# MLP up projections of a two-layer encoder: tokens on partitions in sets of 512 columns, turned by VectorE blocks and SP moves

## The chip, the cores and the metric

The kernel runs on one core of one Trainium2 chip. The metric is the device time in microseconds (us) of one execution, as the median of several runs. The core has TensorE (PE: matrix products into PSUM), VectorE (DVE), ScalarE (ACT), GpSimd (POOL) and SyncE (SP), whose queue issues the DMA transfers here.

## The reference

Two layers on 256 tokens of 1024 channels. Each layer has a token mixer (pooling, attention, gates; not touched here) and then this MLP, with a depthwise convolution of width 3 over the tokens on the branch `a`:

```python
D_MODEL, SEQ, DEPTH, D_FF, CONV_WIDTH, EPS = 1024, 256, 2, 2816, 3, 1e-6

def _conv_ffn(xn, w_up, conv_w, conv_b, w_down):
    a, gval = jnp.split(xn @ w_up, 2, axis=-1)
    a = lax.conv_general_dilated(a, conv_w[:, None, :], window_strides=(1,),
                                 padding=((CONV_WIDTH // 2, CONV_WIDTH // 2),),
                                 dimension_numbers=('NWC', 'WIO', 'NWC'),
                                 feature_group_count=D_FF) + conv_b
    return (jax.nn.gelu(a) * gval) @ w_down

for layer in range(DEPTH):
    h = h + _token_mixer(_rmsnorm(h, norm1[layer]), ...)
    h = h + _conv_ffn(_rmsnorm(h, norm2[layer]), w_up[layer], conv_w[layer], conv_b[layer], w_down[layer])
return _rmsnorm(h, norm_f)
```

All is float32. The kernel computes GELU in its tanh form.

## The kernel before

**Numbers and weights.** Each float32 operand is split into a high and a low part of type fp32r (`wh`, `wl` for weights; two parts of the activations), and a product is three matmuls: high by high, high by low, low by high. Class `Weights` streams the weights in the order in which `use` names the pieces: a load of 1 MB on SP's queue (line 119) fills a tile `raw`, of which three exist; each load is cut in two pieces; ScalarE copies a piece to `wh` (line 179), VectorE subtracts to get `wl` (line 180). Five pairs of `wh` and `wl` exist. `get` hands the next piece to TensorE and has the pieces up to three further ahead split; `_split` issues the loads that fit. A piece counts 128 x 1024 values, whatever its shape: 1024 rows by 128 columns for a column projection, 512 by 256 for rows, and so on. The program issues its instructions in the order of its text; each engine runs its own list in order, and a scheduler between the text and these lists may shift an instruction within its engine's list.

**Two ways to multiply by the up weights.** DFF is 22 chunks of 128 columns; each chunk has an `a` and a `g` half. A *column projection* (`proj`, `two_sums`, lines 485 and 487) holds a 1024 x 128 piece as the fixed operand and streams the 256 tokens: 8 matmuls of 512 columns (both parts of the tokens behind one another), then 8 of 256. Its result has channels on partitions and tokens along the row, as the convolution wants it. *By rows* (`v_sum`, line 582) the tokens are the fixed operand and 512 columns of weights stream; the result has tokens on partitions. One quarter of such a group (one piece, 256 of the 1024 input channels, six matmuls for each of two halves of the tokens, 12 in all) is called a unit below. The tokens stand in two halves, even and odd, `t` = 0 and 1.

**The MLP before.** The `a` of the last four chunks (18 to 21) is computed by rows; its first half is started by `begin_values` at the end of the phase before, to bridge the last norm there. ScalarE copies it out, and VectorE turns it by 32 x 32 blocks that it writes straight to other partitions (`blocks`, line 612). Everything else is a column projection: for each chunk `up(f)` takes `a` (18 times) and `g` (22 times), 40 projections in each layer. `add_up` (lines 507 and 508) lets ScalarE copy one of the two sums out of PSUM and VectorE add the other. Convolution, GELU and the product with `g` follow on ScalarE and VectorE, and the result is split in two parts for the down product.

**Down product and end.** `residual_mm` is a generator with one step per chunk: each of the first 18 steps runs 12 matmuls of 512 columns (lines 512 to 514) into four PSUM tiles; the last four pieces are only held. After them each segment of the result (two of 512 columns for half 0; 512, 256 and 256 for half 1) gets its 12 held matmuls and goes to `Norm.add` (line 417: the sum into `h`; line 419: squares), and in the first layer `fin` of `to_channels` normalises (line 444) and TensorE transposes (line 453); in the last layer `store` scales and writes out. Two chunks of `up` alternate with two steps of `down`, which stay `LAG` = 6 chunks behind.

**Moves.** `cross` (line 604) issues 16 DMAs on SP that carry 32-partition blocks to other partitions, four per step. Attention uses it already (tiles `pt`, 64 KB each, and `way`).

Of the kernel before, what the change touches and what calls it, by code (L numbers as in the profile page):

```python
# [10 lines left out]
F32 = mybir.dt.float32  # L11
F32R = mybir.dt.float32r
AF = mybir.ActivationFunctionType
ALU = mybir.AluOpType
AX = mybir.AxisListType

P = 128
D = 1024
S = 256
# [7 lines left out]
DFF = 2816  # L27
NF = DFF // P
# [7 lines left out]

WARM = (5, 1, 2, 1)
PAIRS = (2, 4, 0, 1, 3, 5)
LAG = 6
VISITS = ((0, 1, 12, 14), (2, 3, 15, 16), (9, 10, 22, 23), (10, 11, 23, 24))  # L40
ENTRY = 4
FIRST = NF - ENTRY
HALVES = (slice(0, 512), slice(512, D))
SEGMENTS = (HALVES, (slice(0, 512), slice(512, 768), slice(768, D)))

# [37 lines left out]
class Weights:  # L83
# [27 lines left out]
    def load(self, upto):  # L111
        while self.n_loaded < min(upto, len(self.loads)):
            src, shape, tag = self.loads[self.n_loaded]
            name = f"raw{self.n_loaded}"
            if tag is None:
                t = self.pool.tile([P, *shape], F32, tag="raw", bufs=self.RAW, name=name)
            else:
                t = self.idle.tile([P, *shape], F32, tag=tag, name=name)
            self.nc.sync.dma_start(out=t, in_=src)
            self.raw[self.n_loaded] = t  # L120
            self.n_loaded += 1

# [84 lines left out]
def encoder(ctx, tc, x, w_in, w_pool, pool_scale, w_a, w_b, w_o, norm1, norm2, w_up, conv_w,  # L207
            conv_b, w_down, rel_bias, norm_f, onehot, edges, out):
    nc = tc.nc
    const = ctx.enter_context(tc.tile_pool(name="const", bufs=1))  # L210
    wpool = ctx.enter_context(tc.tile_pool(name="weights", bufs=1))
    big = ctx.enter_context(tc.tile_pool(name="big", bufs=1))
# [6 lines left out]
    W = Weights(tc, wpool, big)  # L219

    def cols(w, c0):

        src = w[:, c0 : c0 + 256].rearrange("(k p) c -> p k c", p=P)
        return W.add(
            src, (8, 256), [((lambda t, j=j: t[:, :, j * P : (j + 1) * P]), (8, P)) for j in (0, 1)]
        )

    def rows(w, r0, n=2, c0=0, width=1024, tag=None, pieces=2):

        src = w[r0 : r0 + n * P, c0 : c0 + width].rearrange("(k p) c -> p k c", p=P)  # L230
        h = n // pieces
        return W.add(
            src, (n, width), [((lambda t, j=j: t[:, j * h : (j + 1) * h, :]), (h, width)) for j in range(pieces)],
            tag,
        )

    for l in range(DEPTH):
        for g in range(NG):
            c0 = C_V + g * 512
            slots = (("m2", 0, 2), ("m2", 1, 2), ("ybig",), ("at2",)) if g == 0 else ()  # L240
            for j in range(2):
                tag = "k1" if l == 0 and g == 1 and j == 0 else None
                W.use(rows(w_in[l], j * 512, 4, c0, 512, tag), slots[2 * j : 2 * j + 2])
        if l == 0:
            W.n_scaled = len(W.pieces)
        for c in range(3, -1, -1):
            W.use(cols(w_in[l], c * 256))
        for n, c in enumerate(PAIRS):
            q = cols(w_in[l], C_Q + c * 256)
            if n == 1:  # L250
                pool = W.add(
                    w_pool[l].rearrange("g (k p) c -> p (g k) c", p=P), (8, 256),
                    [((lambda t, j=j: t[:, 4 * j : 4 * j + 4, :]), (4, 256)) for j in range(2)],
                )
            k = cols(w_in[l], C_K + c * 256)
            if n == 1:
                k.insert(1, pool[0])
            if n == 2:
                q.insert(1, pool[1])
            W.use(q + k)  # L260
        def half_of(w, c0, half, n):
            for j in range(n):
                W.use(rows(w, j * 512, 4, c0 + half.start, 512))

        for half in HALVES:
            half_of(w_in[l], C_GP, half, 2)
        for half in HALVES:
            half_of(w_a[l], 0, half, 2)
            half_of(w_in[l], C_GA, half, 2)
            half_of(w_b[l], 0, half, 1)  # L270
        for c in range(4):
            W.use(rows(w_o[l], c * 256))
        slots = (("v1",), ("ybig",), ("at2",))
        for j in range(2):
            W.use(rows(w_up[l], j * 512, 4, FIRST * P, 512), slots[2 * j : 2 * j + 2])
        for f in range(0, NF, 2):
            a = cols(w_up[l], f * P) if f < FIRST else []
            g = cols(w_up[l], DFF + f * P)
            W.use([a[0], g[0], a[1], g[1]] if a else g)
            if f >= LAG:  # L280
                W.use(rows(w_down[l], (f - LAG) * P))
        for f in range(NF - LAG, NF, 2):
            W.use(rows(w_down[l], f * P))


    h = const.tile([P, 2, D], F32, name="h")
# [210 lines left out]
    def halves(a):  # L497

        return a.rearrange("p (t m) -> p t m", t=2)

    def in_order(a):

        return a.rearrange("p (m t) -> p t m", t=2)

    def add_up(out, sums):

        nc.scalar.copy(out=out, in_=sums[1])
        nc.vector.tensor_add(out=out, in0=sums[0], in1=out)  # L508
# [65 lines left out]
    def v_tile():  # L574
        return acc.tile([P, 512], F32, tag="acc", name="v_ps")

    def v_sum(ps, x2, t, n, piece, of=4):

        _, (wh, wl) = piece
        passes = [(0, wh, 0), (0, wl, 0), (1, wh, 0), (0, wh, 1), (0, wl, 1), (1, wh, 1)]  # L580
        for m, (part, w, j) in enumerate(passes):
            nc.tensor.matmul(  # L582
                ps, x2[:, 2 * n + j, part, t, :], w[:, j, :], start=(n + m == 0),
                stop=(n == of - 1 and m == 5),
            )
# [21 lines left out]
    def blocks(out, in_):  # L607

        for i in range(4):
            for j in range(4):  # L610
                a, b = slice(32 * i, 32 * i + 32), slice(32 * j, 32 * j + 32)
                nc.vector.transpose(out=out[b, :, :, a], in_=in_[a, :, :, b])
                yield
# [166 lines left out]
    for l in range(DEPTH):  # L780
# [326 lines left out]
        acts = {}  # L1107


        a_last = big.tile([P, ENTRY, S], F32, tag="gates", name="a_last")  # L1110
        a_rows = big.tile([P, 2, ENTRY, P], F32, tag="m2", name="a_rows")

        held, ps = entry
        for t in range(2):
            if t:
                ps = v_tile()
                for n in range(4):
                    v_sum(ps, x2, t, n, held[n])
            nc.scalar.copy(out=a_rows[:, t], in_=ps)
        for i, _ in held:  # L1120
            W.free(i)
        turning = blocks(a_last.rearrange("p f (m t) -> p t f m", t=2), a_rows)

        def up(f):
            w0, w1, w2, b = (prm[:, l, j * NF + f : j * NF + f + 1] for j in range(4))
            if f >= FIRST:
                a = a_last[:, f - FIRST, :]
            else:
                a = sm.tile([P, S], F32, tag="u", name="a")
                add_up(in_order(a), [halves(b) for b in proj(x2)])  # L1130
                next(turning, None)
            sums = proj(x2)
            y = sm.tile([P, S], F32, tag="s", name="y")
            nc.scalar.activation(y, a, AF.Identity, bias=b, scale=w1)  # L1134
            nc.vector.scalar_tensor_tensor(
                out=y[:, 1:], in0=a[:, : S - 1], scalar=w0, in1=y[:, 1:], op0=ALU.mult, op1=ALU.add
            )
            nc.vector.scalar_tensor_tensor(
                out=y[:, : S - 1], in0=a[:, 1:], scalar=w2, in1=y[:, : S - 1],
                op0=ALU.mult, op1=ALU.add,  # L1140
            )
            g = sm.tile([P, 2, P], F32, tag="p", bufs=3, name="g")
            add_up(g, [halves(a) for a in sums])

            c = float(np.sqrt(2.0 / np.pi))
            y2 = sm.tile([P, S], F32, tag="us", name="y2")
            nc.scalar.activation(y2, y, AF.Square, scale=float(np.sqrt(0.044715)))
            nc.vector.scalar_tensor_tensor(  # L1148
                out=y2, in0=y2, scalar=1.0, in1=y, op0=ALU.add, op1=ALU.mult
            )  # L1150
            nc.scalar.activation(y2, y2, AF.Tanh, scale=c)  # L1151
            nc.vector.scalar_tensor_tensor(
                out=y2, in0=y2, scalar=1.0, in1=y, op0=ALU.add, op1=ALU.mult
            )
            nc.vector.scalar_tensor_tensor(
                out=g, in0=in_order(y2), scalar=0.5, in1=g, op0=ALU.mult, op1=ALU.mult
            )
            n = f % NH
            ah, al = (x[n >= HPG][:, n - HPG * (n >= HPG)] for x in (acth, actl))
            nc.scalar.copy(out=ah, in_=g)  # L1160
            nc.vector.tensor_sub(out=al, in0=g, in1=ah.bitcast(F32))
            acts[f] = (ah, al)

        late = {}
# [11 lines left out]
            lambda k: acts[k], NF, lambda *a: late["norm"].add(*a),  # L1176
            fill=begin_values if l + 1 < DEPTH else None,
        )
        for f in range(0, NF, 2):
            up(f)  # L1180
            up(f + 1)
            if f >= LAG:
                next(down)
                next(down)
        if l + 1 < DEPTH:
            x2 = two_parts("x", "x2")
            late["norm"] = Norm(to_channels(x2, mmp, g1))
# [33 lines left out]
```

## Time and profile before

| | |
|---|---|
| median of 3 runs | 870.25 us (870.25 to 870.68) |
| profiled execution, its own time | 870.25 us |
| its span in the trace | 868.5 us |
| mean granted clock of TensorE | 0.998 |
| DMA: mean rate over the span | 193 GB/s |

PE is TensorE's matmuls, PEld its loads of the fixed operand, which overlap them. SPq rows are instructions on SP's queue; a row with x8 stands for eight in succession. In rows of the timeline the first two numbers are the start and the length, both in us. In the list of groups the columns are busy time, mean ns of one, then idle time of the engine just before them and what ended most of it. In the view by tile a row gives the shortest, median and longest duration in ns and the time of the first and last start.

### The profile page before, as it was taken

How to read it: one execution, taken by the hardware profiler on the slowest of the kernel's cores; microseconds unless marked ns; L12 is line 12 of the kernel's file. 1: busy time of each engine (PE TensorE's matmuls, PEld its weight loads, DVE VectorE, ACT ScalarE, POOL GpSimd, SP SyncE). 2: the span in 40 equal slices, each digit the busy share in tenths (PEclk: the TensorE clock that was granted, in tenths of full speed). 3: DMA queues.
4: the chain of work that ended last, by engine and by line, in shares of the span. 5: the costliest groups of instructions: out<-in, count | busy, mean ns of one | idle time of the engine just before them, and what ended most of it. 6: DMA issues, size and time to landing. Idle time of an engine off the chain costs nothing.

```text
span 868.5 us, 12204 instructions
## 1 busy us (share of the span) xinstructions
PE 860.7 (99%) x4554; PEld 740.9 (85%) x4554; DVE 670.5 (77%) x1084; ACT 496.8 (57%) x817; POOL 21.1 (2%) x53
## 2 busy tenths in 40 slices
PE   9999999999999999999999999999999999999997
PEld 7888988888888888888888899888888888888885
DVE  6998795756759997789756968775557799887884
ACT  6755644544646775667545555454445467666662
POOL 2020000000010000000000000000000000000000
PEclk9999999999999999999999999999999999999999
DMA  9676636664745565555626455547558255664631
GB/s 326 210 210 229 223 118 223 189 222 158 270 155 194 185 203 193 197 193 194 242 98 225 163 195 194 173 167 241 186 203 274 96 183 200 223 205 155 198 141 49
DMA packets 116095, 167.23 MB, mean 193 GB/s; under 512 B 4846, under 2 KB 81854, under 8 KB 116036
## 3 DMA queue, kind: packets, MB, share of 16 engines
q1 hardware_dynamic: 115524, 165.12, 56.6%
q0 software_dynamic: 496, 1.33, 0.6%
q8 instruction: 36, 0.59, 0.3%
q14 instruction: 23, 0.19, 0.1%
q10 hardware_dynamic: 16, 0.00, 0.0%
HBM read 160.12 MB, written 1.07 MB: 186 GB/s over the span
## 4 chain that ended last, share of the span: by engine, by line
PE 99%; ACT 0%; POOLq 0%; DVE 0%; issue 0%; POOL 0%; ACTq 0%
PE proj_ps L485 30%; PE rows_ps L582 18%; PE proj_ps L487 16%; PE res_ps L512 6%; PE res_ps L513 6%; PE v_ps L582 6%; PE res_ps L514 6%; PE v_ps L772 3%; PE v_ps L685 1%; PE o_ps L963 1%; PE s_ps L906 1%; PE o_ps L959 1%; PE s_ps L901 1%; PE xt_ps L453 1%; PE pool_ps L479 0%; PE pool_ps L478 0%
## 5 line engine op out<-in xcount | busy, mean ns | idle before, releaser
L180 DVE TENSOR_TENSOR wl<-raw,wh 128x1024 fp32r<-128x1024 f32 x274 | 333.1, 1222 | 121.0 <-ACT wh L179 118.4
L179 ACT CAST wh<-raw 128x1024 fp32r<-128x1024 f32 x274 | 285.6, 1049 | 173.0 <-PE proj_ps L485 64.7
L485 PE MATMUL proj_ps<-x,wh 128*128 128x512 f32 x1152 | 288.4, 392 | 0.0
L485 PEld LDWEIGHTS proj_ps<-x,wh 128*128 128x128 f32 x1152 | 208.2, 189 | 38.0
L487 PEld LDWEIGHTS proj_ps<-x,wl 128*128 128x128 f32 x1152 | 157.2, 190 | 11.3
L487 PE MATMUL proj_ps<-x,wl 128*128 128x256 f32 x1152 | 160.8, 282 | 0.0
L582 PE MATMUL rows_ps<-wh,x 128*128 128x512 f32 x256 | 82.1, 393 | 0.0
L512 PE MATMUL res_ps<-wh,actq 128*128 128x512 f32 (+1 forms) x184 | 70.2, 381 | 0.0
L513 PE MATMUL res_ps<-wl,actq 128*128 128x512 f32 (+1 forms) x184 | 70.1, 381 | 0.0
L514 PE MATMUL res_ps<-wh,actk 128*128 128x512 f32 (+1 forms) x184 | 69.9, 380 | 0.0
L582 PEld LDWEIGHTS rows_ps<-wh,x 128*128 128x128 f32 x256 | 47.9, 188 | 9.7
L582 PE MATMUL rows_ps<-wl,x 128*128 128x512 f32 x128 | 49.9, 389 | 0.0
L514 PEld LDWEIGHTS res_ps<-wh,actk 128*128 128x128 f32 x184 | 34.6, 188 | 6.7
L582 PE MATMUL rows_ps<-wh,po 128*128 128x512 f32 x128 | 40.1, 389 | 0.0
L512 PEld LDWEIGHTS res_ps<-wh,actq 128*128 128x128 f32 x184 | 34.7, 188 | 6.2
L513 PEld LDWEIGHTS res_ps<-wl,actq 128*128 128x128 f32 x184 | 34.7, 188 | 6.0
L1134 ACT ACTIVATE y<-a,prm 128x256 f32<-128x256 f32 x36 | 21.6, 600 | 21.9 <-DVE a L508 21.9
L1151 ACT ACTIVATE y<-y 128x256 f32<-128x256 f32 x44 | 18.3, 416 | 21.4 <-DVE y L1148 21.2
L582 PEld LDWEIGHTS rows_ps<-wh,po 128*128 128x128 f32 x128 | 24.0, 188 | 5.0
L582 PEld LDWEIGHTS rows_ps<-wl,x 128*128 128x128 f32 x128 | 24.1, 188 | 4.8
L512 PE MATMUL res_ps<-wh,m 128*128 128x512 f32 (+1 forms) x72 | 26.9, 374 | 0.0
L419 ACT ACTIVATE junk<-h 128x512 f32<-128x512 f32 (+1 forms) x20 | 10.9, 547 | 27.1 <-DVE h L417 27.1
(209 smaller groups left out, 1155.0 us busy)
## 6 DMA issues: line engine op xcount, KB each, us to landing
raw<-in_w_in_dram SPq DMA_DIRECT2D x58, 1024.0 KB, 5.2
raw<-in_w_up_dram SPq DMA_DIRECT2D x44, 1024.0 KB, 4.9
raw<-in_w_down_dram SPq DMA_DIRECT2D x22, 1024.0 KB, 4.9
raw<-in_w_a_dram SPq DMA_DIRECT2D x8, 1024.0 KB, 5.8
raw<-in_w_o_dram SPq DMA_DIRECT2D x8, 1024.0 KB, 7.1
pt<-rows SPq DMA_DIRECT2D x64, 64.0 KB, 3.7
raw<-in_w_b_dram SPq DMA_DIRECT2D x4, 1024.0 KB
raw<-in_w_pool_dram SPq DMA_DIRECT2D x2, 1024.0 KB
```

The source lines that it names most:

```text
L179: lambda: nc.scalar.copy(out=h, in_=src),
L180: lambda: nc.vector.tensor_sub(out=l, in0=src, in1=h.bitcast(F32)),
L419: nc.scalar.activation(junk[:, 0 : cc.stop - cc.start], h[:, t, cc], AF.Square, scale=D**-0.5, accum_out=ss[:, n : n + 1],)
L485: nc.tensor.matmul(ps, wh(k), x2[:, k], start=(k == 0), stop=False)
L487: nc.tensor.matmul(ps[:, 1], wl(k), x2[:, k, 0], start=False, stop=(k == nk - 1))
L512: nc.tensor.matmul(ps, ah, wh, start=first, stop=False)
L513: nc.tensor.matmul(ps, ah, wl, start=False, stop=False)
L514: nc.tensor.matmul(ps, al, wh, start=False, stop=last)
L582: nc.tensor.matmul(ps, x2[:, 2 * n + j, part, t, :], w[:, j, :], start=(n + m == 0), stop=(n == of - 1 and m == 5),)
L772: nc.tensor.matmul(ps[t], a[:, k, t, :], w[:, j, :], start=(k + m == 0), stop=(k == KD - 1 and m == 2),)
L1134: nc.scalar.activation(y, a, AF.Identity, bias=b, scale=w1)
L1151: nc.scalar.activation(y2, y2, AF.Tanh, scale=c)
```

## The change

All up projections are now by rows. A group is 512 columns: a0 to a4 and g0 to g4 are four chunks of `a` or `g` each, r5 holds the last two chunks of both (two column ranges of 256, loaded by two DMAs from one entry, hence the tuple in `Weights.load`). `ORDER` lists the groups and the steps of the down product, d0 to d4, of four chunks each; chunks 20 and 21 are done in the end. a0 is the one that `begin_values` starts.

`turn_up` turns a finished group: VectorE transposes 32 x 32 blocks out of PSUM, one instruction for each half of the tokens (128 x 512), into `rows`, and `cross` carries the blocks with 16 DMAs of 32 KB on SP's queue to the tile `out`. The moves go out four per unit: `unit`, called after every unit and every down step, takes the next step of the oldest `cross`, and computes each chunk whose number in `CHUNKS` has been passed. `up` finds `a` and `g` turned in SBUF: ScalarE copies `a` into the order of tokens, and the product of GELU and `g` reads `g` where it is. The factor 0.5 moves from that product into the split that follows it, which becomes `scalar.mul` and one `scalar_tensor_tensor`. For each layer 40 column projections of 16 matmuls become 40 units of 12; the matmuls of the down product do not change.

```diff
--- before.py
+++ after.py
@@ -36,10 +36,9 @@
 
 WARM = (5, 1, 2, 1)
 PAIRS = (2, 4, 0, 1, 3, 5)
-LAG = 6
+ORDER = "a0 g0 a1 g1 a2 g2 d0 a3 g3 d1 a4 g4 r5 d2 d3 d4"
+CHUNKS = (13, 15, 17, 19, 21, 23, 25, 27, 29, 31, 33, 35, 41, 43, 45, 47, 53, 54, 56, 57, 58, 60)
 VISITS = ((0, 1, 12, 14), (2, 3, 15, 16), (9, 10, 22, 23), (10, 11, 23, 24))
-ENTRY = 4
-FIRST = NF - ENTRY
 HALVES = (slice(0, 512), slice(512, D))
 SEGMENTS = (HALVES, (slice(0, 512), slice(512, 768), slice(768, D)))
 
@@ -116,7 +115,9 @@
                 t = self.pool.tile([P, *shape], F32, tag="raw", bufs=self.RAW, name=name)
             else:
                 t = self.idle.tile([P, *shape], F32, tag=tag, name=name)
-            self.nc.sync.dma_start(out=t, in_=src)
+            parts = [(t[:, :, j], one) for j, one in enumerate(src)] if type(src) is tuple else [(t, src)]
+            for out, one in parts:
+                self.nc.sync.dma_start(out=out, in_=one)
             self.raw[self.n_loaded] = t
             self.n_loaded += 1
 
@@ -271,16 +272,27 @@
         for c in range(4):
             W.use(rows(w_o[l], c * 256))
         slots = (("v1",), ("ybig",), ("at2",))
-        for j in range(2):
-            W.use(rows(w_up[l], j * 512, 4, FIRST * P, 512), slots[2 * j : 2 * j + 2])
-        for f in range(0, NF, 2):
-            a = cols(w_up[l], f * P) if f < FIRST else []
-            g = cols(w_up[l], DFF + f * P)
-            W.use([a[0], g[0], a[1], g[1]] if a else g)
-            if f >= LAG:
-                W.use(rows(w_down[l], (f - LAG) * P))
-        for f in range(NF - LAG, NF, 2):
-            W.use(rows(w_down[l], f * P))
+        for kind, n in ORDER.split():
+            n = int(n)
+            for j in range(2):
+                if kind == "d":
+                    W.use(rows(w_down[l], (4 * n + 2 * j) * P))
+                elif kind == "r":
+                    src = w_up[l][j * 512 : (j + 1) * 512].rearrange("(k p) c -> p k c", p=P)
+                    c0 = (4 * n * P, 4 * n * P + DFF)
+                    W.use(
+                        W.add(
+                            tuple(src[:, :, c : c + 256] for c in c0), (4, 2, 256),
+                            [
+                                ((lambda t, j=j: t[:, 2 * j : 2 * j + 2].rearrange("p k h c -> p k (h c)")), (2, 512))
+                                for j in (0, 1)
+                            ],
+                        )
+                    )
+                else:
+                    p = rows(w_up[l], j * 512, 4, (kind == "g") * DFF + 4 * n * P, 512)
+                    W.use(p, slots[2 * j : 2 * j + 2] if (kind, n) == ("a", 0) else ())
+        W.use(rows(w_down[l], (NF - 2) * P))
 
 
     h = const.tile([P, 2, D], F32, name="h")
@@ -1107,29 +1119,40 @@
         acts = {}
 
 
-        a_last = big.tile([P, ENTRY, S], F32, tag="gates", name="a_last")
-        a_rows = big.tile([P, 2, ENTRY, P], F32, tag="m2", name="a_rows")
-
-        held, ps = entry
-        for t in range(2):
-            if t:
-                ps = v_tile()
-                for n in range(4):
-                    v_sum(ps, x2, t, n, held[n])
-            nc.scalar.copy(out=a_rows[:, t], in_=ps)
-        for i, _ in held:
-            W.free(i)
-        turning = blocks(a_last.rearrange("p f (m t) -> p t f m", t=2), a_rows)
+        turned, ways = {}, []
+
+        def turn_up(key, ps, tag):
+
+            if not ways:
+                for own in ("at2", "xn"):
+                    t = big.tile([P, 2, 4, 2, 4, 32], F32, tag=own, name="up_" + own)
+                    ways.append([t[:, 0], t[:, 1]])
+                ways.append([])
+            rows = ways[0].pop(0)
+            ways[0].append(rows)
+            if tag is None:
+                out = ways[1].pop(0)
+                ways[1].append(out)
+            else:
+                out = big.tile([P, 4, 2, 4, 32], F32, tag=tag, name="up_turned")
+            for t in range(2):
+                nc.vector.transpose(
+                    out=rows[:, :, t].rearrange("p j c r -> p c j r"),
+                    in_=ps[t].rearrange("p (c j r) -> p c j r", c=4, j=4),
+                )
+            ways[2].append(cross(out, rows))
+            turned[key] = out.rearrange("p i t c r -> p c t i r")
+
+        def blocks_in_order(a):
+
+            return a.rearrange("p (i r t) -> p t i r", i=4, t=2)
 
         def up(f):
             w0, w1, w2, b = (prm[:, l, j * NF + f : j * NF + f + 1] for j in range(4))
-            if f >= FIRST:
-                a = a_last[:, f - FIRST, :]
-            else:
-                a = sm.tile([P, S], F32, tag="u", name="a")
-                add_up(in_order(a), [halves(b) for b in proj(x2)])
-                next(turning, None)
-            sums = proj(x2)
+            n, c = divmod(f, 4)
+            av, gv = (turned["r", n][:, j + c] if n == 5 else turned[k, n][:, c] for k, j in (("a", 0), ("g", 2)))
+            a = sm.tile([P, S], F32, tag="u", name="a")
+            nc.scalar.copy(out=blocks_in_order(a), in_=av)
             y = sm.tile([P, S], F32, tag="s", name="y")
             nc.scalar.activation(y, a, AF.Identity, bias=b, scale=w1)
             nc.vector.scalar_tensor_tensor(
@@ -1139,8 +1162,6 @@
                 out=y[:, : S - 1], in0=a[:, 1:], scalar=w2, in1=y[:, : S - 1],
                 op0=ALU.mult, op1=ALU.add,
             )
-            g = sm.tile([P, 2, P], F32, tag="p", bufs=3, name="g")
-            add_up(g, [halves(a) for a in sums])
 
             c = float(np.sqrt(2.0 / np.pi))
             y2 = sm.tile([P, S], F32, tag="us", name="y2")
@@ -1152,13 +1173,14 @@
             nc.vector.scalar_tensor_tensor(
                 out=y2, in0=y2, scalar=1.0, in1=y, op0=ALU.add, op1=ALU.mult
             )
-            nc.vector.scalar_tensor_tensor(
-                out=g, in0=in_order(y2), scalar=0.5, in1=g, op0=ALU.mult, op1=ALU.mult
-            )
+            g = sm.tile([P, 2, P], F32, tag="p", bufs=3, name="g")
+            nc.vector.tensor_mul(out=g.rearrange("p t (i r) -> p t i r", i=4), in0=blocks_in_order(y2), in1=gv)
             n = f % NH
             ah, al = (x[n >= HPG][:, n - HPG * (n >= HPG)] for x in (acth, actl))
-            nc.scalar.copy(out=ah, in_=g)
-            nc.vector.tensor_sub(out=al, in0=g, in1=ah.bitcast(F32))
+            nc.scalar.mul(out=ah, in_=g, mul=0.5)
+            nc.vector.scalar_tensor_tensor(
+                out=al, in0=g, scalar=0.5, in1=ah.bitcast(F32), op0=ALU.mult, op1=ALU.subtract
+            )
             acts[f] = (ah, al)
 
         late = {}
@@ -1176,12 +1198,38 @@
             lambda k: acts[k], NF, lambda *a: late["norm"].add(*a),
             fill=begin_values if l + 1 < DEPTH else None,
         )
-        for f in range(0, NF, 2):
-            up(f)
-            up(f + 1)
-            if f >= LAG:
-                next(down)
-                next(down)
+        count, chunk = 0, 0
+
+        def unit():
+            nonlocal count, chunk
+            count += 1
+            if ways and ways[2] and next(ways[2][0], "end") == "end":
+                ways[2].pop(0)
+                if ways[2]:
+                    next(ways[2][0])
+            while chunk < NF and CHUNKS[chunk] < count:
+                up(chunk)
+                chunk += 1
+
+        for kind, n in ORDER.split():
+            if kind == "d":
+                for _ in range(4):
+                    next(down)
+                    unit()
+                continue
+            if (kind, n) == ("a", "0"):
+                held, ps = entry
+                ps = [ps, v_tile()]
+                for k in range(4):
+                    v_sum(ps[1], x2, 1, k, held[k])
+                    unit()
+                for i, _ in held:
+                    W.free(i)
+            else:
+                ps = by_rows(x2, 4, unit)
+            n = int(n)
+            turn_up((kind, n), ps, None if kind == "g" else ("gates", "v0")[n % 2])
+        assert chunk == NF
         if l + 1 < DEPTH:
             x2 = two_parts("x", "x2")
             late["norm"] = Norm(to_channels(x2, mmp, g1))
```

## The prediction

> **What bounds the kernel now.** First the page, for which engine sets the end.
>
> ```profile
> span 868.5 us, 12204 instructions
> PE 860.7 (99%) x4554; PEld 740.9 (85%) x4554; DVE 670.5 (77%) x1084; ACT 496.8 (57%) x817; POOL 21.1 (2%) x53
> PEclk9999999999999999999999999999999999999999
> PE 99%; ACT 0%; POOLq 0%; DVE 0%; issue 0%; POOL 0%; ACTq 0%
> ```
>
> The chain of waits is TensorE for 99% of the span, at an undisturbed clock. Busy matmuls overlap, so a gap could hide in that figure; the table by stretch, here for layer 0 from the first column projection of the MLP to the start of layer 1, and the timeline of TensorE in one round show that none does.
>
> ```profile
> core 0: us, PE busy (x) PEld busy (x) DVE busy (x) ACT busy (x) POOL busy (x), PEclk, DMA share, GB/s
> 263.66:436.18 172.52, 172.52 (x926) 149.29 (x924) 150.27 (x266) 112.76 (x201) 1.61 (x4) 1.00 0.59 201
> ...
> 347.02 1.98 PE L485 MATMUL proj_ps<-x,wh 128*128 128x512 f32 x8
> 348.83 1.12 PE L487 MATMUL proj_ps<-x,wl 128*128 128x256 f32 x8
> 349.79 2.00 PE L485 MATMUL proj_ps<-x,wh 128*128 128x512 f32 x8
> ...
> 358.17 0.40 PE L512 MATMUL res_ps<-wh,actq 128*128 128x512 f32 x1
> ...
> 363.41 0.39 PE L514 MATMUL res_ps<-wh,actk 128*128 128x512 f32 x1
> 363.63 0.39 PE L485 MATMUL proj_ps<-x,wh 128*128 128x512 f32 x1
> ```
>
> TensorE is busy in 172.52 of 172.52 us. Four column projections stand between 347.02 and 358.17: 11.15 us, 2.79 each. Then 24 matmuls of 512 columns take 358.17 to 363.63: 5.46 us, 0.2275 each. So the MLP costs what TensorE needs to stream it, and each idle moment that the change brings to TensorE is paid in full.
>
> **The stream: a gain.** A column projection streams 8 x 512 and 8 x 256 columns in 16 matmuls; a quarter of a group by rows (a "unit") streams the same columns in 12 matmuls of 512. At 0.2275 a unit is 2.73 us, a group of four 10.92 against 11.15. Ten groups (g0 to g4, a1 to a4, r5) replace 40 projections in each layer; a0 was by rows already. 20 groups x 0.23 = **-4.6 us**. The 18 matmuls of each down step do not change.
>
> The Trainium skill ("TensorE: Matmul & The Clock Gate", section "Wait — 56ns, not 53.3ns?") gives a warm matmul a fixed cost of about 2.5 ns besides its columns. Four matmuls fewer in each of 80 units would then save 0.8 us, not 4.6, an estimate from that page; the trace disagrees, with 58 ns saved per unit by its own pitches.
>
> **VectorE and ScalarE: less work, another order.**
>
> ```profile
> L180 DVE TENSOR_TENSOR wl<-raw,wh 128x1024 fp32r<-128x1024 f32 x60 | 73.4, 1223 | 12.0 <-ACT wh L179 11.4
> L508 DVE TENSOR_TENSOR g<-proj_ps,g 128x256 f32<-128x256 f32 x22 | 9.2, 417 | 0.0
> L508 DVE TENSOR_TENSOR a<-proj_ps,a 128x256 f32<-128x256 f32 x18 | 7.5, 419 | 0.0
> L612 DVE STREAM_TRANSPOSE a_last<-a_rows 32x256 f32<-32x256 f32 x16 | 7.0, 436 | 0.3
> L507 ACT COPY g<-proj_ps 128x256 f32<-128x256 f32 x22 | 7.9, 358 | 0.0
> ...
> L1059 DVE STREAM_TRANSPOSE way<-th x2: 1239/1239/1239, 204.0 to 630.5; 128x1024 f32<-128x1024 f32 x2
> L417 DVE TENSOR_TENSOR h<-res_ps,h x20: 415/683/692, 242.8 to 862.0; 128x512 f32<-128x512 f32 x12, 128x256 f32<-128x256 f32 x8
> ```
>
> Per layer VectorE loses 40 sums and 16 block transposes (9.2 + 7.5 + 7.0 = 23.7 us) and gets 22 transposes of 128x512 out of PSUM. The trace has none of that form: half of the 128x1024 one is 0.62 us, the 128x512 sum out of PSUM takes up to 0.69. I take 0.69, 15.2 us in all. ScalarE loses 40 copies and gets 22. Neither engine's total is the danger.
>
> The order is. The built changed kernel's list of VectorE instructions (no times in it; against the trace of before, such a list agrees with the order that ran) has this at the end of group a3, whose results are rows_ps_3165 and rows_ps_3166; unit 32 is its last, and wl114 belongs to unit 33, the first of g3 (line numbers of the changed kernel):
>
> ```
> 372 L181 wl112_3129<-raw56, wh112
> 373 L181 wl113_3168<-raw56, wh113
> ...
> 383 L1139 StreamTranspose up_at2<-rows_ps_3165 [waits DMA, PE]
> 386 L1139 StreamTranspose up_at2<-rows_ps_3166 [waits PE]
> 387 L181 wl114_3184<-raw57, wh114 [waits DMA, Activation]
> ```
>
> So the low part of unit 33's weights is made only after a transpose that waits for the last matmul of unit 32, and TensorE's list for unit 33 is two matmuls with wh114, then one with wl114. Elsewhere the low parts of two or three units ahead stand before the transpose. The same happens at the end of a4 (wl126) and twice in layer 1 (wl262, wl274). What is queued behind the waiting transpose is the subtraction; who waits for that is TensorE.
>
> ```profile
> 412.35 0.42 DVE L508 TENSOR_TENSOR g<-proj_ps,g 128x256 f32<-128x256 f32 x1
> 412.68 0.41 DVE L1152 SCALAR_TENSOR_TENSOR y<-y,y 128x256 f32<-128x256 f32 x1
> ...
> 861.73 0.28 PE L514 MATMUL res_ps<-wh,actk 128*128 128x256 f32 x1
> 862.04 0.42 DVE L417 TENSOR_TENSOR h<-res_ps,h 128x256 f32<-128x256 f32 x1 [0.24 <-PE res_ps L514]
> ```
>
> From the start of unit 32's last matmul: 0.39 until its result, 0.03 until VectorE starts (862.01 to 862.04), 0.61 for the transpose (0.69 less the 0.08 by which a successor starts early, 412.35 + 0.42 against 412.68), 1.22 for the subtraction, 0.05 back to TensorE (my estimate, as short as the 0.03): 2.30. TensorE fills 3 x 0.2275 = 0.68. It idles 1.62, four times: 6.5 us. The bounds are 1.5 (a 0.62 transpose) and 1.8 (no overlap). At the end of g4 only the first transpose, 6 matmuls earlier, stands before wl130: 2.30 - 1.37 - 0.68 = 0.25, twice 0.5. Together **+7.0** (6.2 to 7.8).
>
> **The ends of the two MLPs.** TensorE's list also changes there: the list has the last held steps, k = 18 and 19, for all segments first and k = 20 and 21 after them. Before, each segment ended with its own 12 matmuls of 512, so the two of token half 0 were done 5.5 us and more ahead of the end; now 1.4 us of matmuls stand between one segment and the next.
>
> ```profile
> 429.57 0.39 PE L514 MATMUL res_ps<-wh,actk 128*128 128x512 f32 x1
> 430.17 0.68 DVE L417 TENSOR_TENSOR h<-res_ps,h 128x512 f32<-128x512 f32 x1
> 432.63 0.48 DVE L444 SCALAR_TENSOR_TENSOR xn<-h,rstd,gain 128x256 f32<-128x256 f32 x1 [1.78 <-POOL rstd L431]
> 433.95 0.60 PE L453 MATMUL xt_ps<-ident,xn 128*128 128x128 f32 x4
> ...
> 859.39 0.68 DVE L417 TENSOR_TENSOR h<-res_ps,h 128x512 f32<-128x512 f32 x1
> 860.72 0.42 DVE L417 TENSOR_TENSOR h<-res_ps,h 128x256 f32<-128x256 f32 x1
> ```
>
> Layer 0: from the last matmul of half 0 (429.57) to the first quarter of the normalised row (432.63 + 0.48) pass 3.54 us. TensorE then has, besides that matmul's own 0.23, 6 matmuls of 0.23 and 6 of 0.12 before it needs it: 2.3. It idles **1.2** (0 if VectorE's chain shortens, 2.5 if it comes late from its last chunks). Layer 1: VectorE needs 1.33 us for each 512-wide segment (859.39 to 860.72), and three of them now end within 1.8 us of matmuls, so it is still on them when the last matmul ends. It starts about 2.7 before the start of that matmul, needs 4.0 for three segments, 0.4 for a scaling and about 1 for the quarters: its last sum starts near 2.5 after it, against 0.31 before (862.04 less 861.73). I take **+2.0** (0.5 to 2.5).
>
> **SP's queue: costed at nothing, barely.** In runs of groups it has per two units (5.46 us of TensorE) one load and eight moves.
>
> ```profile
> 167.48 0.53 SPq L119 DMA_DIRECT2D raw<-in_w_in_dram  x1
> 168.05 6.18 SPq L604 DMA_DIRECT2D pt<-rows  x8
> 174.32 0.53 SPq L119 DMA_DIRECT2D raw<-in_w_b_dram  x1
> ...
> 205.34 7.49 SPq L604 DMA_DIRECT2D way<-way  x12
> ...
> SPq L604 <- DMA raw<-in_w_in_dram: 3.7, 4, 1.3
> ...
> raw<-in_w_up_dram SPq DMA_DIRECT2D x44, 1024.0 KB, 4.9
> ```
>
> A move costs 0.62 (7.49 by 12), so eight and a load need 5.0 + 0.57 = 5.6 us, already over 5.46; where the moves also waited for a load to land, the round took 6.84 (167.48 to 174.32, with moves of 64 KB; these have 32). I take 6.1. The longest run, a0 to g2, has 11 rounds after its first load: 11 x 0.64 = 7 us late at its end. A load is issued about 18 us ahead of its use (7 units less 0.3), of which 4.9 to 6.2 go for landing and 2.3 for the split: 10 left. The cover is that look-ahead, and gaps without moves (a3, a4 and most down steps) refill it. At 6.84 it would be gone: 15.2 - 10 = 5 us per layer.
>
> **Sum.** -4.6 + 7.0 + 1.2 + 2.0 = +5.6 on 868.5: a span of 874.1. The profiled execution took 870.25 with this span, 1.75 outside it, and 870.25 is also the median of the runs. Forecast **875.9 us**, slower; its own range is 872 to 879.
>
> **Rivals.**
> - *The stream alone decides* (not slower): the low parts come in time and the ends stay hidden. 870.25 - 4.6 = 865.7. For it: the gain is the surest term, and VectorE's total falls by 8 us. Against it: the list itself puts wl114 behind the wait. It decides if the four waits and the two ends together cost under 2.9 us. Chance 0.10.
> - *Waits and gain cancel*: the ends are hidden and the waits shorter, about 1.2 each: 870.25 - 4.6 + 5 = 870.7. Chance 0.13.
> - *SP becomes the bound*: rounds of 6.84. TensorE runs out of weights near the end of a0 to g2, 5 us per layer, of which the wait after a3 would have been 1.6 anyway: 875.9 + 2 x 3.4 = 882.7. For it: the one round in the trace with this pattern. Against it: half the bytes. Chance 0.12.
> - *The fixed cost of the page is right*: the gain shrinks by 3.8 and the time is 879.7, by the page's rule; chance 0.02, since the pitches are measured.
>
> **How the numbers follow.** The forecast has 0.63. A measurement of this kernel tells about 0.2% (1.7 us) from no change. Below 868.5 lies the first rival: faster 0.10; 868.5 to 872 the second: same 0.13; the rest, 0.77, is slower. The range for 8 in 10 reaches from 868 into the cancelling case up to 881.5, short of the SP case.
>
> **What would show it.** Right: TensorE idles some 1.6 us at the first unit of g3 and of g4 in both layers, put down to VectorE's subtraction, and nearly nowhere else in the MLP; units pitch at 2.73; the transposes take about 0.69; some 2 us more pass from the last matmul to the end. Wrong: no idle at g3 and g4 (then about 865.7), waits of ScalarE's split for w_up loads with SP late (then SP is the bound), transposes out of PSUM well over 1 us, or a pitch of groups by rows other than 0.2275.

## The result and the profile after

The changed kernel takes 878.67 us (median of 4 runs, 877.04 to 879.53) against 870.25 us (870.13 to 870.68): a ratio of 1.0094, with a 95% interval of 1.0076 to 1.0111. It is slower by 8.4 us; the forecast was 875.9 us in a range of 868 to 881.5.

From the page of the changed kernel, and its waits by engine (what TensorE waited for: us in total, times, the longest):

```profile
span 876.9 us, 11882 instructions
PE 858.1 (98%) x4234; PEld 725.0 (83%) x4234; DVE 653.6 (75%) x1016; ACT 481.6 (55%) x777; POOL 21.2 (2%) x53
PE 85%; DVE 6%; DMA 5%; ACT 1%; SPq 1%; issue 1%; POOL 0%; POOLq 0%; DVEq 0%; ACTq 0%
L1139 DVE STREAM_TRANSPOSE up_at<-rows_ps 128x512 f32<-128x512 f32 x40 | 28.2, 710 | 28.6 <-PE rows_ps L594 23.1
```

```profile
PE rows_ps L594 <- DVE wl L181: 5.9, 4, 1.5
PE xt_ps L465 <- DVE xn L456: 2.7, 1, 2.7
```

The chain of waits, 99% TensorE before, now runs 6% over VectorE and 5% over DMA. VectorE is less busy than before, 653.6 us against 670.5, and yet TensorE waits for it. The list of waits leaves out TensorE's shorter stops, and a time of idling is not yet a loss; so the account is made from starts of matmuls that both kernels have: the first of the mixer's output product in each layer, and the last of all. A pitch is the time from one start to the next.

```profile
227.98 0.39 PE L512 MATMUL res_ps<-wh,m 128*128 128x512 f32 x1
...
654.43 0.39 PE L512 MATMUL res_ps<-wh,m 128*128 128x512 f32 x1
```

The same two in the changed kernel, and its last matmul:

```profile
227.81 0.39 PE L524 MATMUL res_ps<-wh,m 128*128 128x512 f32 x1
...
659.43 0.39 PE L524 MATMUL res_ps<-wh,m 128*128 128x512 f32 x1
...
867.90 0.28 PE L526 MATMUL res_ps<-wh,actk 128*128 128x256 f32 x1
```

| stretch | before | after | difference |
|---|---|---|---|
| start to layer 0's output product | 227.98 | 227.81 | -0.17 |
| from there to layer 1's (MLP 0, boundary, mixer 1) | 426.45 | 431.62 | +5.17 |
| from there to the last matmul (MLP 1) | 207.30 | 208.47 | +1.17 |
| last matmul to the end of the span | 6.77 | 9.00 | +2.23 |

Where the stops lie shows in TensorE's timeline at the end of a3, beside VectorE's there:

```profile
339.36 0.84 PE L594 MATMUL rows_ps<-wh,x 128*128 128x512 f32 x3
341.66 0.50 PE L594 MATMUL rows_ps<-wl,x 128*128 128x512 f32 x1 [1.46 <-DVE wl L181]
342.00 0.63 PE L594 MATMUL rows_ps<-wh,x 128*128 128x512 f32 x2
```

```profile
338.43 0.72 DVE L1139 STREAM_TRANSPOSE up_at<-rows_ps 128x512 f32<-128x512 f32 x1 [3.81 <-PE rows_ps L594]
339.07 0.38 DVE L1173 SCALAR_TENSOR_TENSOR y<-y,y 128x256 f32<-128x256 f32 x1
339.37 0.47 DVE L1158 SCALAR_TENSOR_TENSOR y<-a,prm,y 128x255 f32<-128x255 f32 x1
339.79 0.72 DVE L1139 STREAM_TRANSPOSE up_at<-rows_ps 128x512 f32<-128x512 f32 x1
340.43 1.18 DVE L181 TENSOR_TENSOR wl<-raw,wh 128x1024 fp32r<-128x1024 f32 x1
```

VectorE stands idle for 3.81 us in front of the first transpose, while a subtraction that TensorE will need stands behind the second. ScalarE's cast of that piece was long done, as its timeline shows, so the subtraction could have run in the idle time.
```profile
335.16 1.99 ACT L180 CAST wh<-raw 128x1024 fp32r<-128x1024 f32 x2
```

TensorE's four starts from 339.36 to 342.00 hold 2.64 us where four pitches are 0.91: 1.73 lost. At the end of a4 (idle 1.49) it is 1.77, at the end of g4 (idle 0.11) 0.37: 3.88 in layer 0. In layer 1 the same three stops lose 3.89, so 7.77 in all.

At the boundary of the layers a second thing is added to the idle time. TensorE's timeline, then the table by stretch (its column PEclk is the granted clock):

```profile
434.72 0.28 PE L526 MATMUL res_ps<-wh,actk 128*128 128x256 f32 x1
437.65 0.66 PE L465 MATMUL xt_ps<-ident,xn 128*128 128x128 f32 x2 [2.65 <-DVE xn L456]
...
441.16 1.18 PE L594 MATMUL v_ps<-m,x 128*128 128x512 f32 x4
```

```profile
434.70:437.60 2.90, 0.30 (x3) 0.09 (x1) 1.86 (x5) 2.31 (x9) 1.50 (x4) 0.90 1.04 396
437.60:441.10 3.50, 3.45 (x19) 3.48 (x20) 2.21 (x6) 0.59 (x1) 0.28 (x1) 0.59 0.32 120
```

After 2.65 us without work TensorE was granted only 0.59 of its clock in the next 3.5 us: its matmuls of 256 columns stand 0.21 apart there instead of 0.12. From 434.72 to 441.16 pass 6.44 us. In the first experiment below the same instructions take 3.91 at full clock with a pause of 1.64 from start to start where 0.12 would do, so 2.39 without one: the boundary costs 4.05. Of these 2.81 are the stop (2.93 from start to start, less 0.12), and 1.24 is what the instructions behind it take longer (3.51 us against 2.27).

### The profile page after: what moved, and what is told of

It is laid out like the page before. It is cut to its first block, busy times and chain, and to the rows that moved or that the text cites. A ratio compares the mean times of both kernels' runs of the same rounds, so it can differ in the third digit from the quotient of the medians.

```text
span 876.9 us, 11882 instructions
## 1 busy us (share of the span) xinstructions
PE 858.1 (98%) x4234; PEld 725.0 (83%) x4234; DVE 653.6 (75%) x1016; ACT 481.6 (55%) x777; POOL 21.2 (2%) x53
## 4 chain that ended last, share of the span: by engine, by line
PE 85%; DVE 6%; DMA 5%; ACT 1%; SPq 1%; issue 1%; POOL 0%; POOLq 0%; DVEq 0%; ACTq 0%
PE rows_ps L594 37%; PE proj_ps L497 13%; PE proj_ps L499 7%; PE v_ps L594 6%; PE res_ps L524 4%; PE res_ps L525 4%; PE res_ps L526 4%; DVE wl L181 3%; PE v_ps L784 2%; DMA raw<-in_w_up_dram 2%; PE v_ps L697 1%; DMA up_turned<-up_at 1%; SPq L616 1%; DMA up_xn<-up_at 1%; PE o_ps L975 1%
## 5 line engine op out<-in xcount | busy, mean ns | idle before, releaser
L594 PE MATMUL rows_ps<-wh,x 128*128 128x512 f32 x896 | 280.4, 390 | 0.0
L594 PEld LDWEIGHTS rows_ps<-wh,x 128*128 128x128 f32 x896 | 168.1, 188 | 34.6
L594 PE MATMUL rows_ps<-wl,x 128*128 128x512 f32 x448 | 175.1, 391 | 6.1 <-DVE wl L181 5.9
L497 PE MATMUL proj_ps<-x,wh 128*128 128x512 f32 x512 | 128.6, 393 | 0.0
L497 PEld LDWEIGHTS proj_ps<-x,wh 128*128 128x128 f32 x512 | 92.1, 189 | 16.5
L594 PEld LDWEIGHTS rows_ps<-wl,x 128*128 128x128 f32 x448 | 84.1, 188 | 25.7 <-DVE wl L181 8.7
L499 PEld LDWEIGHTS proj_ps<-x,wl 128*128 128x128 f32 x512 | 69.9, 190 | 5.1
L499 PE MATMUL proj_ps<-x,wl 128*128 128x256 f32 x512 | 71.5, 282 | 0.0
L1139 DVE STREAM_TRANSPOSE up_at<-rows_ps 128x512 f32<-128x512 f32 x40 | 28.2, 710 | 28.6 <-PE rows_ps L594 23.1
L1180 ACT ACTIVATE actq<-g 128x256 fp32r<-128x256 f32 x44 | 17.8, 412 | 37.6 <-DVE g L1177 37.5
```

The costliest lines, as they stand in the source:

```text
L497: nc.tensor.matmul(ps, wh(k), x2[:, k], start=(k == 0), stop=False)
L499: nc.tensor.matmul(ps[:, 1], wl(k), x2[:, k, 0], start=False, stop=(k == nk - 1))
L594: nc.tensor.matmul(ps, x2[:, 2 * n + j, part, t, :], w[:, j, :], start=(n + m == 0), stop=(n == of - 1 and m == 5),)
L1139: nc.vector.transpose(out=rows[:, :, t].rearrange("p j c r -> p c j r"), in_=ps[t].rearrange("p (c j r) -> p c j r", c=4, j=4),)
L1180: nc.scalar.mul(out=ah, in_=g, mul=0.5)
```

## Experiments

Each kernel is the changed kernel with one edit. The runs of the kernel before beside them had medians of 869.62 us (first four experiments), 869.88 (next three) and 869.58 (last).

**1. The low part ahead of the transposes.** Only VectorE's order at the ends of a3, g3, a4 and g4 changes; `W.low` keeps the subtraction of each piece, and its line numbers are up to 4 higher. SP's and POOL's lists are those of the changed kernel; besides VectorE's order, one instruction of ScalarE and two matmuls shift by a few places in each layer.

```diff
+            with ExitStack() as queued:
+                if W.n_got in W.low:
+                    queued.enter_context(tc.issue_after(W.low[W.n_got].ins))
                 for t in range(2):
                     nc.vector.transpose(
...
```

> The changed kernel with one edit: VectorE's two transposes of a group are queued behind the subtraction that makes the low weight part of the next unit; SP's queue and all else stay. Theory A (the order on VectorE makes the four long and two short waits): the idle moments of TensorE at the first units of g3, g4 and r5 vanish, 3.9 us of pitch per layer, 7.75 in all: 878.67 - 7.75 = 870.9 us (870 to 872). Theory B (SP's queue is late, and the low parts would not have come earlier anyway): the waits stay and are put down to ScalarE's split or to a load; 877 us or more.

Measured: 867.49 us, ratio 0.9977 (0.9968 to 0.9987). All waits for a low part are gone, and what is left is the boundary, in the waits (the second is at the program's start) and in the timeline:

```profile
PE xt_ps L466 <- DVE xn L457: 1.4, 1, 1.4
PE gain_ps L347 <- DVE ones L333: 1.0, 1, 1.0
```

```profile
430.20 0.28 PE L527 MATMUL res_ps<-wh,actk 128*128 128x256 f32 x1
431.84 0.41 PE L466 MATMUL xt_ps<-ident,xn 128*128 128x128 f32 x2 [1.36 <-DVE xn L457]
...
434.11 0.71 PE L595 MATMUL v_ps<-m,x 128*128 128x512 f32 x2
```

```profile
431.80:435.30 3.50, 3.46 (x25) 3.32 (x26) 3.35 (x7) 1.50 (x4) 0.26 (x1) 1.00 0.22 83
```

(The last row is of the table by stretch.) Theory A holds: an order of instructions alone, with the same work on the same queues, made the change slower than the kernel before instead of faster. The run gained 3.4 us more than expected. 2.5 of it are the boundary (3.91 us instead of 6.44), where the idle time fell from 2.65 to 1.36 and the clock stayed at 1.00; another 0.6 is from ahead of the MLP, in code that isn't changed (227.24 against 227.81; in the kernels here that start scatters from 227.24 to 228.29). The shorter pause goes with a longer lead of the last moves, those for chunks 20 and 21: on SP's queue they end at 407.71 here, 22.5 us ahead of the matmul at 430.20, against 416.38 and 18.3 us in the changed kernel.

```profile
405.30 2.41 SPq L617 DMA_DIRECT2D up_turned<-up_at  x4
```

```profile
413.97 2.41 SPq L616 DMA_DIRECT2D up_turned<-up_at  x4
```

(The first row is of the experiment, the second of the changed kernel.)

**2. The closing in its old order.** `end` is the last matmul of the segment before; only in the MLP (`n == NF`). `one` now returns its last matmul.

```diff
+                with ExitStack() as queued:
+                    if end and n == NF:
+                        queued.enter_context(tc.issue_after(end.ins))
                     for j, (i, part) in enumerate(held):
-                        one(part, res, t, cc, c0 != 0 and j == 0, j == hold - 1)
+                        last = one(part, res, t, cc, c0 != 0 and j == 0, j == hold - 1)
+                end = last
```

> The changed kernel with one edit: at the end of each MLP TensorE's matmuls of a segment (k = 18 to 21) are queued behind the last matmul of the segment before, as the order was in the kernel before. Theory A (the compressed order alone costs the 2.65 us at the layer boundary and the 2.2 us of tail): both vanish, 878.67 - 4.9 = 873.8 us. Theory B (chunks 20 and 21 are late, since their moves stand behind others in SP's queue, and the compressed order only follows that): in the changed kernel the last segments start at 856.9 us and the last part of chunk 21 is made until 860.7, so TensorE now waits about 2.5 us in front of k = 20 in each layer and the ends become short again: 878 to 879 us, about the same.

Measured: 877.89 us, 0.8 less than the changed kernel. Its waits:

```profile
PE res_ps L524 <- ACT actq L1184: 1.5, 2, 1.2
PE res_ps L526 <- DVE actk L1185: 1.1, 2, 0.6
```

Theory B holds: both ends are short again (6.4 us from the last matmul to the end of the span, against 9.00), but the old order moves the idle time in front of chunks 20 and 21, which are late. The waits are shorter than the 2.5 us that B expected, 1.74 us in layer 0 and 0.91 in layer 1; in layer 0 a lowered clock comes on top (last section). So the compressed order is no cost of its own. That the planner (the scheduler that sets each engine's list) chose it because the chunks are late fits this, and is not shown by it.

**3. Half of the moves on POOL's queue.**

```diff
-                nc.sync.dma_start(out=out[b, i], in_=in_[a, j])
+                (nc.gpsimd if j >= 2 and len(out.shape) == 5 else nc.sync).dma_start(out=out[b, i], in_=in_[a, j])
```

> The changed kernel with two of the four moves of each step issued by POOL's queue and two by SP's. The planner then orders the low parts ahead of the transposes and the closing segment by segment by itself. Theory A (the moves on SP's one queue are behind all losses: by the late loads that the planner reckons with, and by the late chunks): no wait is left, the gain of the stream stays, 870.25 - 4.6 = 865.7 us (865 to 868). Theory B (the moves cost by themselves: VectorE's transposes, 16 transfers per group beside the loads, POOL's slower issue): 870 us or more.

Measured: 867.46 us, ratio 0.9975 (0.9965 to 0.9984). (The condition also holds for 16 moves outside the MLP.) In the list of VectorE's instructions the planner now puts the low part of unit 33 and of the three units after it ahead of a3's transposes by itself, and it closes segment by segment. The trace agrees for VectorE:

```profile
337.90 1.22 DVE L181 TENSOR_TENSOR wl<-raw,wh 128x1024 fp32r<-128x1024 f32 x1 [0.36 <-ACT wh L180]
339.05 1.30 DVE L1139 STREAM_TRANSPOSE up_at<-rows_ps 128x512 f32<-128x512 f32 x2
```

No wait of TensorE is left in either MLP, and the chain of waits has its two long stretches of units:

```profile
263.34 54.40 PE rows_ps L594 x240
...
687.25 54.40 PE rows_ps L594 x240
```

240 matmuls in 54.40 us are 0.2267 each, 2.72 a unit. The last matmul starts at 855.76, 5.97 ahead of the kernel before, but the span ends only 3.1 earlier. What comes between is POOL's drain at the program's end (duration in ns: least, median, longest), first of the kernel before, then of this one:

```profile
L1216 POOLq DRAIN  x3: 40/102/1358, 863.4 to 868.2; - x3
```

```profile
L1264 POOLq DRAIN  x3: 40/102/7151, 857.5 to 865.1; - x3
L1264 SPq DRAIN  x3: 7/7/7, 861.3 to 864.9; - x3
```

SP has come to its first drain at 861.3; POOL's lasts from 857.5 for 7.15 us, so until 864.6.

**4. The bad order on the relieved queue.** As 3, and the low parts of unit 33 and 45 are queued behind the last transpose of a3 and a4. The edit is wider than that: in these two groups it also shortens how far ahead pieces are split (`W.get(of - 1 - n)`).

```diff
+            piece = W.get() if ahead else W.get(of - 1 - n)
...
+            if key[0] == "a" and key[1] in (3, 4):
+                W.queue_behind([turn], 1)
```

> As the run with half of the moves on POOL, but the low parts of the first units of g3 and g4 are held back behind the last transpose of a3 and a4, as in the changed kernel. SP's queue is as relieved as there. Theory A (order on VectorE): four waits of about 1.75 us of pitch come back, 7 us above the run without this edit (about 872.7). Theory B (SP's lateness made the waits): no more than 1 us above it.

Measured: 871.7 us, 4.2 above run 3. This lies between the two expectations, a little nearer to A, and the experiment is not clean: TensorE's list changed as well. With the low parts late, the planner put matmuls of the down step into the gap, and TensorE now waited there for a cast:

```profile
340.42 1.21 PE L524 MATMUL res_ps<-wh,actq 128*128 128x512 f32 x4 [0.69 <-ACT wh L180]
```

So the order costs time with SP relieved too; its price of 1.75 a wait was not reproduced.

**5. A quarter of the moves on POOL, or on ScalarE; none at all.** One move of four (`j == 3`) goes to `nc.gpsimd` or to `nc.scalar`, in the MLP alone; the third kernel leaves the moves out (`cross` is not called), so that what follows is computed from blocks in the wrong places. A group has 16 moves and the two MLPs have 22 groups, so a quarter is 88 moves and a half 176; the expectations of this and the next experiment count 80 and 160.

> The changed kernel with one of the four moves of each step on POOL's queue, three on SP's (80 moves in all on POOL; moves outside the MLP stay on SP). In the run with half of the moves on POOL, TensorE had no wait left and its last matmul started at 855.76 us, 5.97 us earlier than in the kernel before; but POOL's drain at the end of the program took 7.15 us (857.48 to 864.63) against 1.35, and the other queues had ended at 861.40. Theory A (the drain grows with the moves that POOL issued, 5.8 us for 176 of them, 0.033 each): 80 moves make it about 4.0 us, over by 861.5, hidden behind the last store: 867.46 - 3.2 = 864.3 us. Theory B (a drain of fixed length as soon as POOL's queue carries moves): 867.5 us.

> The same quarter of the moves on ScalarE's queue in place of POOL's. VectorE's order of low parts and transposes is the same as with a quarter on POOL. Theory A (ScalarE has room for 80 issues, and no drain follows): 864.2 us. Theory B (an issue holds ScalarE as it holds SP, 0.6 us, and waits there in line for a transpose, so that casts and chunks come late): 866 us or more, with waits of TensorE for ScalarE's split.

> The changed kernel without the moves: VectorE's transposes write the tiles that the chunks read, and the blocks are not carried to other partitions, so the product of GELU and g and all after it is computed from blocks in the wrong places. SP's queue has the loads alone. Theory A (the moves cost nothing but what their lateness does to the order): no wait, the gain of the stream, ends as in the kernel before: a span of 855.8 + 6.75 = 862.5 and 864.3 us. Theory B (the moves also take something from loads or from VectorE that even the run with half on POOL paid): a last matmul before 854.5 us, 863 us or less.

Measured: 869.3 us with a quarter on POOL (ratio 0.9995, 0.9986 to 1.0004), 865.5 us with a quarter on ScalarE (0.995, 0.9937 to 0.9964), 863.88 us without moves (0.9931, 0.9917 to 0.9944). The drains of the first two:

```profile
L1265 POOLq DRAIN  x3: 40/102/8539, 858.1 to 867.2; - x3
```

```profile
L1265 POOLq DRAIN  x3: 40/93/1357, 858.8 to 863.2; - x3
```

The drain doesn't grow with the moves: it took 8.54 us after 88 moves on POOL's queue and 7.15 after 192 (176 of the MLPs and the 16 others), so theory A of that run falls. B is nearer, though a second part was missed: TensorE's last matmul starts at 856.43, 0.7 later than in run 3, with 1.0 us of idle at the boundary. On ScalarE the same orders cost no drain, and the expectation of 864.2 was missed by 1.3, as 1.65 us of idle at the boundary are left. Without moves the end is where A put it (last matmul at 855.78, within 0.02 of run 3): beyond the orders, the late chunks and the drain, the moves cost nothing that the time shows. The version with a quarter on ScalarE beats both kernels.

**6. Half of the moves on ScalarE.**

> Two of the four moves of each step on ScalarE's queue. With a quarter there, one wait is left, 1.65 us for the normalised row at the layer boundary, since SP still falls somewhat behind and chunks 20 and 21 come late; with half of the moves on POOL, and without moves, that wait is gone. Theory A (what is left of the loss is SP's lateness at the ends of the MLPs): the wait goes and the time is that of the kernel without moves, 863.9 us, within 0.5. Theory B (160 issues crowd ScalarE): 866 us or more, with new waits of TensorE for ScalarE.

Measured: 901.55 us, ratio 1.0375 (1.036 to 1.0389). B by far. What ScalarE and TensorE waited for:

```profile
ACT wh L180 <- DMA up_xn<-up_at: 25.4, 9, 6.1
```

```profile
PE res_ps L525 <- DVE wl L181: 8.3, 16, 1.2
PE res_ps L524 <- ACT actq L1181: 5.6, 3, 2.6
```

By the profile's releasers, casts of weights stood up to 6.1 us behind moves that waited on ScalarE for an earlier move to land. TensorE's granted clock also fell to 0.50 twice, over 10.2 us from 434.4 and 6.8 us from 878.1. How the loss divides between the waits and the clock was not worked out. With a quarter none of this showed; the edge between 88 and 176 issues was not searched.

## Why the prediction was right, and what it mis-sized

| term | predicted | measured |
|---|---|---|
| stream of units | -4.6 | -5.48 |
| low parts behind transposes | +7.0 | +7.77 |
| boundary of the layers | +1.2 | +4.05 |
| tail after the last matmul | +2.0 | +2.23 |
| before the MLP, unchanged code | 0 | -0.17 |
| sum | +5.6 | +8.4 |

The second term is measured at the six stops, the third at the boundary (both above). The stream's is what the two MLP stretches leave: 5.17 - 3.88 - 4.05 = -2.76 in layer 0 and 1.17 - 3.89 = -2.72 in layer 1.

- *The stream* was right and taken too small by a rounded pitch: a unit is 12 x 0.2267 = 2.72, not 2.73, and 80 x 0.01 is nearly all of the difference. By the fixed cost of 2.5 ns from the Trainium skill ("TensorE: Matmul & The Clock Gate", section "Wait — 56ns, not 53.3ns?") it would have been 0.8, an estimate from that page; the trace disagrees a second time.
- *The order on VectorE* was right in place, cause and number. The forecast counts in pitches: from 339.36 to 341.66 pass 2.30 us, as forecast, and less three pitches of 0.2267 that is 1.62. The four long stops are 1.62 to 1.66 on this count (forecast 1.62), the two short ones 0.27 (0.25). The profile's 1.46 to 1.49 and 0.11 are smaller because they begin at the modelled end of the last matmul, 0.39 after its start. The transposes take 0.71 (forecast 0.69). The term came out larger because the matmul behind each stop starts 0.33 or 0.34 after the one in front, not 0.23: some 0.11 a stop that the forecast didn't have. Experiment 1 shows the cause, since little but the order differs.
- *The layer boundary* is the mis-sized step. The wait for the first quarter of the normalised row was named, with 2.5 as its upper bound and 1.2 taken; it idled 2.65, and the lowered clock after it was not in the account. 2.85 us are missing here; the other four deviations (-0.88, +0.77, +0.23, -0.17) cancel, which is luck.
- *The tail* was right in size: VectorE's last operation starts 4.90 us after the start of the last matmul, 2.36 before.

```profile
864.09 0.48 DVE L468 TENSOR_SCALAR xn<-xn,rstd 128x512 f32<-128x512 f32 x1 [1.16 <-POOL rstd L431]
```

```profile
872.80 0.49 DVE L480 TENSOR_SCALAR xn<-xn,rstd 128x512 f32<-128x512 f32 x1 [1.16 <-POOL rstd L443]
```

- *SP's queue, costed at nothing*, held only for direct waits. The round of eight moves and a load is as estimated, here 5.9 to 6.1 us from load to load against 5.44 of TensorE:

```profile
316.65 0.53 SPq L120 DMA_DIRECT2D raw<-in_w_up_dram  x1
317.30 5.29 SPq L616 DMA_DIRECT2D up_turned<-up_at  x8
322.69 0.53 SPq L120 DMA_DIRECT2D raw<-in_w_up_dram  x1
...
328.62 0.52 SPq L120 DMA_DIRECT2D raw<-in_w_up_dram  x1
...
334.76 0.53 SPq L120 DMA_DIRECT2D raw<-in_w_up_dram  x1
```

  TensorE never waits for a load. But experiments 3 and 5 show that the other three losses hang on how many moves go through this queue: with a part of them elsewhere, or none, the planner orders the low parts first and the closing by segments, though with a quarter elsewhere 1.0 and 1.65 us of idle time stay at the boundary. That the planner does so because it reckons with late loads was only argued. The prediction gave the three terms as separate, and put the two ends down to TensorE's order alone; experiment 2 shows that another order saves next to nothing while the chunks are late.
- *The rivals.* The stream alone (865.7) is nearly what the kernel without moves shows, 863.88, so its mechanism was right and its condition wasn't met. Waits and gain don't cancel (870.7): the waits were not 1.2 but 1.62 and more, and the ends were not hidden. SP as the bound (882.7) named the right queue and the wrong victim.

## What to carry to other kernels

Before the time is looked at, read in each engine's list what stands behind an instruction that waits for the bottleneck engine: here two transposes in front of one subtraction, twice in each layer, cost more than 320 saved matmuls gave, and swapping them turned 878.67 into 867.49 us. A queue that is only a little late can cost nothing by itself and still decide orders elsewhere, so test it by moving part of its work to another queue. Watch what that queue adds: POOL's drain ate about half of the gain in one run and nearly all in another, and ScalarE carried 88 issues well and 176 very badly.

## What the runs showed of the hardware that was not expected

- A pause of TensorE can cost more than its length. After 2.65 us idle the granted clock was 0.59 over the next 3.5 us, while after 1.36 (experiment 1), 1.46 and 1.49 (the changed kernel) and 1.65 (a quarter on ScalarE) it stayed at 1.00. In experiment 2 two pauses, 1.23 and 0.51 us, within 3 us were enough (timeline, then table by stretch):

```profile
427.87 0.51 PE L524 MATMUL res_ps<-wh,actq 128*128 128x512 f32 x1 [1.23 <-ACT actq L1184]
...
429.11 0.50 PE L526 MATMUL res_ps<-wh,actk 128*128 128x512 f32 x1 [0.51 <-DVE actk L1185]
```

```profile
429.90:433.30 3.40, 3.40 (x10) 2.65 (x9) 3.40 (x4) 1.05 (x2) 0.00 (x0) 0.51 1.00 320
```

  The Trainium skill ("TensorE: Matmul & The Clock Gate", section "Part 1: The HAM clock gate") puts the return to half the clock after at least one idle window of some 3.4 us. The low stretch is about as long as that window, but the pause that brought it was shorter.
- POOL's drain at the end lasted 1.36 us with POOL's few DMAs of before, and 7.15 to 8.54 us with 88 moves or more, though the last of these had been issued long before: in run 3 by 823.1, 34 us ahead of the drain. The cause stays open.
